# The first group's embedding product moved to the start of the program, and the last group's norm moved to VectorE

## The chip, the cores and the metric

The kernel runs on one core of a Trainium2 chip. The metric is the device time of one execution in microseconds (us). Times are medians over a few executions. The views of the trace below come from one profiled execution of the kernel before the change.

The engines are called PE (TensorE matmuls), PEld (its weight loads, which overlap with the matmuls), DVE (VectorE), ACT (ScalarE), POOL (GpSimd) and SP (SyncE, which here issues nearly all of the DMAs). TensorE runs at one of two clocks, 2.4 GHz or 1.2 GHz; the profile gives the granted share (1.00 or 0.50).

## The reference, cut to what matters

One layer on x with 2048 frames of 1024 features, all in float32:

```python
h = layer_norm(x)
q, k, v, gate, ... = split(h @ w_in)          # chunked attention and gated linear attention
mixer = concat(attention * silu, gla * silu) @ w_out
r = alpha * h + mixer
ple = p @ w_ple                               # "embedding product": p is 2048 x 256, w_ple 256 x 1024
y = r + sigmoid(r @ w_ple_gate + b) * ple
out = layer_norm(y)                           # "final norm"
```

The embedding product needs only the inputs p and w_ple. Its result is used at the end of the layer, in the gate.

## The kernel before

**Tiling.** The frames are cut into two superblocks (`sb` = 0, 1) of 1024 frames, and each into two groups (`g` = 0, 1) of 512. Everything is kept transposed, features on the partitions. A float32 product is made of three matmuls on parts of the operands: high by high, low by high, and high by low (`hh`, `hl` for the data, `whi`, `wlo` for the weights). A matmul has 128x512 columns, except for the last slabs of the last group, which have 256.

**Order.** For each superblock `gla_phase`, `attn_phase` and `out_phase` follow each other. The first `gla_phase` begins with `head()`, which norms the first x blocks, transposes them (`ln_T`: PE transposes, ACT evacuates as `t` on line 229, DVE splits into `hh` and `hl` on lines 151 and 152), and splits the first weight slabs. `out_phase` runs the output projection (slabs o0 to o7; the evacuation `ev_r` on lines 1171 to 1176 makes r and splits it), and then for each group the embedding product (48 matmuls with the left operands `whi` and `wlo` of two slabs of w_ple and the right ones `pTh`, `pTl`; evacuated as `ple` on line 1182) and eight gate slabs (`ev_y`, lines 1192 to 1201). `p_T(g)` loads p, transposes it with 8 PE transposes (line 1160) and splits it.

**Weights.** A slab is loaded raw by SP (`w_load`, `wraw`), cast to its high part by ACT (line 286) or DVE (line 284), and its low part is made by DVE (line 291). If the slab is used again, both parts go to DRAM (`wkept`) and are fetched from there later (`w_fetch`).

**What sets the order on an engine.** After every four matmuls `gemm` calls `tick()`, which runs evacuations that were put off and advances a "side" generator (`set_side`), whose `yield n` says after how many ticks it goes on. In `head()` and in the last slabs of the last group the order on DVE, ACT and POOL is the order in which the code is written (`manual_schedule`); elsewhere a scheduler orders the instructions. Each engine works in order. SP's DMAs use eight semaphores in turn, so each waits until the one eight places ahead of it has landed.

**The end.** `ln_last` is the final norm of the last group, which runs as a side generator beside the last slabs: transposes of the outputs `y`, statistics (line 414), scale and offset (lines 366, 367, 458, 474), stores. Some of its multiplications and additions run on POOL.

Of the kernel before, what the change touches and what calls it, by code (L numbers as in the profile page):

```python
# [26 lines left out]
F32 = mybir.dt.float32  # L27
# [17 lines left out]
def hymba_layer_kernel(  # L45
# [211 lines left out]
    def w_load(i, pool=pool_r, tag="r"):  # L257
        if i >= len(order) or i in wt or not first_use(i):
            return
        wt[i] = w_tile(pool, F32, i, "wraw", tag)  # L260
        queued.append(nc.sync.dma_start(wt[i], order[i]).ins)
# [73 lines left out]
    I = lambda *ns: [("i", n) for n in ns]  # L335
    for sb in range(NSB):
        keys += [("v", 0), ("v", 1)] + I(GQ, GK)
        keys += I(GV + 2, GV + 3, GQ + 1, GK + 1)
        keys += I(GG, GG + 1)
        for h in (0, 2):  # L340
            keys += I(*[n + h for n in (AK, AV, AV + 1, AQ, AG, AK + 1, AQ + 1, AG + 1)])
        keys += I(GG + 2, GG + 3)
        keys += [("o", k) for k in range(8)]
        for g in range(2):
            keys += [("e", 0), ("e", 1)] + [("g", k) for k in range(8)]
# [57 lines left out]
    def ln_last(sb, g, rows, ys, pst):  # L403
# [24 lines left out]
        def fin(b, hf, eng, mul=None):  # L428
            norm(b, hf)
            ln_store(sb, g, b, hf, y[b][hf], rows, eng, mul)  # L430

        for b in range(4):
            ps = pst(0)
            part(b, range(4), ps)
            nc.scalar.activation(y[b][0], ps, AF.Copy)
            yield 3
        yield 2
# [4 lines left out]
        yield 9  # L442
        for b in range(2):
            part(b, range(6, 8), pss[b])
            yield 1.5
        scale(0)
        yield 3
        fin(0, 1, nc.gpsimd)
        fin(0, 0, nc.gpsimd)
        yield 1  # L450
# [3 lines left out]
        fin(1, 0, nc.gpsimd, nc.gpsimd)  # L454
        yield 3.5
        norm(1, 1)
        yield 100
        TT = lambda eng, b, hf, i, op: eng.tensor_tensor(y[b][hf], y[b][hf], rows[2 * i + hf], op=op)
        for b in range(2, 4):
            part(b, [6], pss[b])  # L460
        TT(nc.vector, 1, 1, 0, OP.mult)
        for b in range(2, 4):
            part(b, [7], pss[b])
# [5 lines left out]
        TT(nc.gpsimd, 1, 1, 1, OP.add)  # L469
        ln_put(sb, g, 1, 1, y[1][1])  # L470
        for b in (1, 0):
            nc.scalar.activation(y[2 + b][0], y[2 + b][0], AF.Identity, bias=nm[:, b:b + 1], scale=r[:, b:b + 1])
# [4 lines left out]
        TT(nc.gpsimd, 3, 0, 0, OP.mult)  # L477
        TT(nc.vector, 2, 0, 0, OP.mult)
        TT(nc.vector, 2, 0, 1, OP.add)
        ln_put(sb, g, 2, 0, y[2][0])  # L480
        TT(nc.vector, 3, 0, 1, OP.add)
        ln_put(sb, g, 3, 0, y[3][0])
# [14 lines left out]
    khist = dram.tile([4, 2, 128, 512], F32, name="khist")  # L497
    vhist = dram.tile([2, 4, 2, 128, 512], F32, name="vhist")
# [12 lines left out]
    def gla_phase(sb):  # L511
# [234 lines left out]
        def head(idx):  # L746
# [34 lines left out]
            with tc.manual_schedule(engines={E.DVE, E.Activation, E.Pool}):  # L781
# [11 lines left out]
                w_split(0, "dve")  # L793
# [17 lines left out]
                w_split(2, "lo")  # L811
                w_split(3, "act")
                w_split(3, "lo")
                w_load(4)
                w_load(5)
# [324 lines left out]
    def out_phase(sb):  # L1140
# [66 lines left out]
        set_side(p_T(0), scale=3)  # L1207
        for s in range(0, 8, 2):
            for g in range(2):
                if s == 6 and g == 1 and nxt:  # L1210
                    xs = x_load(sb + 1, 0)
                for n in range(2):
                    gemm(wos[s + n], 8, 0, lambda k, g=g: (mh[k][g], ml[k][g]),
                         ev_r(s + n, g), g == 1)
        end_sides()
        end_pend()
        for g in range(2):
            pw = take(2)
            for s in range(8):
                gemm(pw[s // 4], 2, 2 * (s % 4), lambda k: pT[k], ev_ple(s), s % 4 == 3)  # L1220
# [7 lines left out]
            else:  # L1228
# [49 lines left out]
    edge["x"] = x_load(0, 1)  # L1278
# [65 lines left out]
```

## Time and profile before

| | before |
|---|---|
| median of 3 runs | 1376.54 us (1371.83 to 1377.86) |
| profiled execution | 1372.83 us |
| its span, first to last instruction | 1371.0 us |
| PE busy in the span | 1332.9 us (97%) |
| DVE busy, ACT busy | 739.2 us (54%), 562.1 us (41%) |
| mean granted TensorE clock | 0.992 |

The profiled execution's own time is 1.8 us more than its span, and it lies 3.7 us below the median of the three runs. The busy times say that PE works nearly without a pause; only where PE is idle, or at half clock, can time be won without taking work from it.

### The profile page before, as it was taken

Reading aid. Unit: us, or ns where it says so; the run is one execution under the profiler, and the core shown is the slowest. Engines: PE = TensorE matmul, PEld = TensorE weight load, DVE = VectorE, ACT = ScalarE, POOL = GpSimd, SP = SyncE. Lnnn points to the kernel's source line nnn. Section 1 sums busy time; section 2 is a strip of 40 time slices with the busy share of each in tenths; the row PEclk is TensorE's granted clock in tenths of the full one; section 3 lists DMA queues with packets and bytes.
Section 4 is the critical chain, followed back from the end, with each engine's and each line's share of the span. In section 5 each row is a group of like instructions: output and inputs, shape, how many; then the busy total and the mean of one; then the engine's idle time right before and its main releaser. Section 6 shows DMA issues by size and latency. Waiting matters only on the chain.

```text
span 1371.0 us, 21628 instructions
## 1 busy us (share of the span) xinstructions
PE 1332.9 (97%) x8440; PEld 1132.1 (83%) x8440; DVE 739.2 (54%) x1641; ACT 562.1 (41%) x1064; POOL 154.1 (11%) x233
## 2 busy tenths in 40 slices
PE   6999999999999999999999999999999999999995
PEld 5888888888888888888898988888888887888875
DVE  7755625554455745546884552455445555332286
ACT  4655525444454522524544542444344443112222
POOL 1000001211111100000100010121211120000012
PEclk9999999999999999999999999999999999999998
DMA  8360525241523335766613131322222213235551
GB/s 320 59 197 21 212 72 215 72 162 33 208 96 137 131 133 195 273 220 231 204 69 117 55 118 62 131 80 79 70 101 93 79 40 130 93 119 195 201 184 63
DMA packets 60271, 180.60 MB, mean 132 GB/s; under 512 B 6864, under 2 KB 8968, under 8 KB 60168
## 3 DMA queue, kind: packets, MB, share of 16 engines
q1 hardware_dynamic: 59648, 177.64, 36.9%
q10 hardware_dynamic: 520, 1.57, 1.1%
q8 instruction: 67, 1.10, 0.3%
q14 instruction: 36, 0.29, 0.1%
HBM read 116.14 MB, written 63.05 MB: 131 GB/s over the span
## 4 chain that ended last, share of the span: by engine, by line
PE 89%; DVE 5%; ACT 3%; DMA 1%; issue 1%; POOL 0%; SPq 0%; ACTq 0%; DVEq 0%; POOLq 0%
PE proj L317 56%; PE proj L917 7%; PE PT L1027 5%; PE PV L1050 5%; PE proj L557 5%; PE S L994 3%; PE S L992 2%; PE O L704 1%; DMA wraw<-in_wi_dram 1%; PE kvp L657 1%; PE O L700 1%; DVE ysb L397 1%; PE CN L679 1%; PE CN L317 0%; DVE ysb L399 0%
## 5 line engine op out<-in xcount | busy, mean ns | idle before, releaser
L317 PE MATMUL proj<-hh,whi 128*128 128x512 f32 (+1 forms) x912 | 358.4, 393 | 1.3 <-ACT glr L574 0.7
L317 PE MATMUL proj<-hh,wlo 128*128 128x512 f32 (+1 forms) x912 | 357.3, 392 | 0.0
L317 PE MATMUL proj<-hl,whi 128*128 128x512 f32 (+1 forms) x912 | 353.7, 388 | 0.0
L317 PEld LDWEIGHTS proj<-hh,whi 128*128 128x128 f32 x912 | 172.5, 189 | 30.3 <-issue 1.0
L317 PEld LDWEIGHTS proj<-hl,whi 128*128 128x128 f32 x912 | 172.4, 189 | 29.4
L317 PEld LDWEIGHTS proj<-hh,wlo 128*128 128x128 f32 x912 | 172.3, 189 | 29.1
L1002 ACT ACTIVATE P<-P,s 128x640 f32<-128x640 f32 (+4 forms) x128 | 97.5, 761 | 159.6 <-DVE s L1001 101.3
L1010 POOL TENSOR_SCALAR P<-P,s 128x640 f32<-128x640 f32 (+4 forms) x128 | 96.1, 750 | 486.5 <-DVE s L1009 393.7
L998 DVE CUSTOM_DVE_ANT_0 P<-S,bias 128x640 f32<-128x640 f32 (+4 forms) x128 | 94.7, 740 | 103.8 <-PE S L994 100.6
L317 PE MATMUL proj<-mh,whi 128*128 128x512 f32 x256 | 99.9, 390 | 0.0
L317 PE MATMUL proj<-mh,wlo 128*128 128x512 f32 x256 | 99.6, 389 | 0.0
L159 POOL TENSOR_TENSOR rstd<-v,nhalf 128x1 f32<-128x1 f32 (+2 forms) x44 | 33.2, 761 | 573.7 <-DVE v L157 524.9
L1027 PE MATMUL PT<-ident,P 128*128 128x128 f32 x560 | 83.8, 276 | 0.0
L291 DVE TENSOR_TENSOR wlo<-wraw,whi 128x1024 fp32r<-128x1024 f32 (+1 forms) x46 | 56.0, 1224 | 49.7 <-ACT whi L286 48.1
L1032 ACT ACTIVATE PT<-PT 128x384 f32<-128x384 f32 (+2 forms) x128 | 59.3, 464 | 50.8 <-PE PT L1027 50.1
L1027 PEld LDWEIGHTS PT<-ident,P 128*128 128x128 f32 x560 | 65.3, 140 | 14.2 <-issue 5.1
L317 PE MATMUL proj<-ml,whi 128*128 128x512 f32 x192 | 75.1, 391 | 0.0
L557 PE MATMUL proj<-whi,hl 128*128 128x272 f32 (+1 forms) x256 | 74.7, 296 | 0.0
L557 PE MATMUL proj<-whi,hh 128*128 128x272 f32 (+1 forms) x256 | 74.0, 296 | 0.7 <-ACT glr L574 0.7
L917 PE MATMUL proj<-whi,hh 128*128 128x256 f32 x256 | 74.4, 291 | 0.0
L888 DVE SCALAR_TENSOR_TENSOR ql<-proj,qh 64x512 fp32r<-64x512 f32 x64 | 44.0, 688 | 53.2 <-ACT qh L885 51.5
L917 PE MATMUL proj<-wlo,hh 128*128 128x256 f32 x256 | 72.3, 283 | 0.0
(216 smaller groups left out, 2389.9 us busy)
## 6 DMA issues: line engine op xcount, KB each, us to landing
whi<-wkept SPq DMA_DIRECT2D x64, 512.0 KB, 3.6
wlo<-wkept SPq DMA_DIRECT2D x64, 512.0 KB, 4.4
wkept<-whi SPq DMA_DIRECT2D x44, 512.0 KB, 2.7
wkept<-wlo SPq DMA_DIRECT2D x44, 512.0 KB, 3.3
wraw<-in_wi_dram SPq DMA_DIRECT2D x26, 512.0 KB, 5.1
x<-in_x_dram SPq DMA_DIRECT2D x32, 256.0 KB, 5.7
out_dram<-ysb SPq DMA_DIRECT2D x32, 256.0 KB, 2.1
bias<-relrows SPq DMA_DIRECT2D x32, 144.0 KB, 2.8
```

What stands on the lines that cost most here:

```text
L291: nc.vector.tensor_tensor(lo, raw, hi.bitcast(F32), op=OP.subtract)
L317: nc.tensor.matmul(ps[:, cols], lhsT=l[:, c0 + k, :], rhs=rhs(k)[m][:, cols], start=(j == 0), stop=(j == n - 1))
L557: nc.tensor.matmul(ps[:, c0:c0 + nw], lhsT=h[k][g][:, b * 128:(b + 1) * 128], rhs=W[k // 4][m][:, k % 4, :], start=(n == 0), stop=(n == 23))
L888: nc.vector.scalar_tensor_tensor(ql[h][o, :], ps[r, :], QSCALE, qh[h][r, :].bitcast(F32), op0=OP.mult, op1=OP.subtract)
L917: nc.tensor.matmul(ps[:, bb * 256:bb * 256 + 256], lhsT=h[k][g][:, c], rhs=W[k // 4][m][:, k % 4, :], start=(k == 0 and n == 0), stop=(k = ...
L994: nc.tensor.matmul(ps[:, d0:d0 + n1], lhsT=ll, rhs=kt[:, c0:c0 + n1], start=False, stop=True)
L998: nc.vector.tensor_tensor_reduce(P[:, :ncol], ps[:, 512 - n_prev:512 + n_cur], bias[pr, h][:, 640 - ncol:640], 1.0, -3e38, OP.add, OP.max, ...
L1002: nc.scalar.activation(P[:, :ncol], P[:, :ncol], AF.Exp, bias=s4[:, 1:2], scale=1.0, accum_out=s4[:, 2:3])
L1010: nc.gpsimd.tensor_scalar(P[:, :ncol], P[:, :ncol], s4[:, 3:4], 1.0, op0=OP.mult, op1=OP.mult)
L1027: nc.tensor.transpose(ps[:, b, :], P[:, (b0 + b) * 128:(b0 + b + 1) * 128], ident)
L1032: nc.scalar.activation(pt[:, ks, cs], ps[:, :nb, :], AF.Copy)
L1050: nc.tensor.matmul(pv[r, qp * 256 + c0:qp * 256 + c1], lhsT=V[pr, gi][:, kb * 128 + 64 * h:kb * 128 + 64 * h + 64], rhs=pt[h][:, b - k0, c ...
```

## The change

The change has three parts.

1. **Start.** The embedding product of superblock 0, group 0 becomes the first work of the program. p of this group (two DMAs of 256 KB) and the two slabs of w_ple (now also under the key "f") are loaded ahead of and between the x blocks. `head()` first splits p and w_ple, then runs eight products of six matmuls each; the norm, transposes and splits of the first two x blocks (`first()`) run as their side generator. ACT evacuates each of the eight results, and SP stores it to DRAM (`pled`, 256 KB each). ACT instead of DVE now casts the first v slab. The raw loads of the slabs GQ and GK and of the second group's x are issued later on SP.
2. **Middle.** In `out_phase` of superblock 0, `p_T(0)` and the 48 matmuls of group 0 are gone. Eight loads bring `ple` back from DRAM; SP issues them behind the eight loads of the next x. The w_ple slabs are first used under "e" at group 1, so the raw load, split and store that stood at group 0 now stand there.
3. **End.** In `ln_last` all scale and offset work is on DVE, none on POOL. Its start is put off from 32 to 35, and its pauses (`yield`) become shorter.

```diff
+    slab.update({("f", k): wple[k] for k in range(2)})
+    keys += [("f", 0), ("f", 1)]
...
-            keys += [("e", 0), ("e", 1)] + [("g", k) for k in range(8)]
+            keys += [("e", k) for k in range(2) if sb or g] + [("g", k) for k in range(8)]
...
-        def fin(b, hf, eng, mul=None):
+        def fin(b, hf):
             norm(b, hf)
-            ln_store(sb, g, b, hf, y[b][hf], rows, eng, mul)
+            ln_store(sb, g, b, hf, y[b][hf], rows, nc.vector)
...
-            yield 3
-        yield 2
+            yield 2.4
...
-        yield 9
+        yield 4.4
         for b in range(2):
             part(b, range(6, 8), pss[b])
-            yield 1.5
+            yield 0.8
         scale(0)
         yield 3
-        fin(0, 1, nc.gpsimd)
-        fin(0, 0, nc.gpsimd)
-        yield 1
+        for b in range(2):
+            fin(b, 1)
+            yield 1.5
+        for b in range(2):
+            fin(b, 0)
+            yield 1.8
...
-        fin(1, 0, nc.gpsimd, nc.gpsimd)
-        yield 3.5
-        norm(1, 1)
         yield 100
...
-        TT(nc.gpsimd, 3, 0, 0, OP.mult)
-        TT(nc.vector, 2, 0, 0, OP.mult)
-        TT(nc.vector, 2, 0, 1, OP.add)
...
+        for b in range(2, 4):
+            TT(nc.vector, b, 0, 0, OP.mult)
+            TT(nc.vector, b, 0, 1, OP.add)
...
+            def p_T():
+
+                for k in range(2):
+                    ps = bank()
+                    for b in range(4):
+                        nc.tensor.transpose(ps[:, b * 128:(b + 1) * 128],
+                                            edge["p0"][b // 2][:, b % 2 * 256 + k * 128:b % 2 * 256 + k * 128 + 128],
+                                            ident)
+                    pT[k] = U("pTh", F32R), U("pTl", F32R)
+                    nc.scalar.activation(pT[k][0], ps, AF.Copy)
+                    nc.vector.tensor_tensor(pT[k][1], ps, pT[k][0].bitcast(F32), op=OP.subtract)
+
+            def ev_f(s):
+                def ev(ps):
+                    t = U("ple")
+                    nc.scalar.activation(t, ps, AF.Copy)
+                    nc.sync.dma_start(pled[s], t)
+                return ev
...
+                w_split(F[1], "lo")
+                w_load(idx[3])
+                edge["x"] = x_load(0, 1)
+                w_split(V[0], "act")
+                yield
                 for k, _ in enumerate(ln_T(0, xs, bank, range(0, 2))):
                     if k == 1:
-                        w_split(1, "act")
-                w_split(0, "lo")
-                w_split(1, "lo")
-                w_split(2, "act")
+                        w_split(V[1], "act")
+                    if k == 4:
+                        w_split(V[0], "lo")
+                    yield
+
+            with tc.manual_schedule(engines={E.DVE, E.Activation, E.Pool}):
+                w_split(F[0], "dve")
+                p_T()
+                w_split(F[0], "lo")
+                w_load(idx[2])
+                w_split(F[1], "act")
+                set_side(first(), delay=-1)
+                for s in range(8):
+                    gemm(F[s // 4], 2, 2 * (s % 4), lambda k: pT[k], ev_f(s), False, lo_last=True)
+                end_sides()
+                end_pend()
+                for f in F:
+                    del wt[f]
+                w_split(V[1], "lo")
+                w_split(idx[2], "act")
...
-        set_side(p_T(0), scale=3)
+        if sb:
+            set_side(p_T(0), scale=3)
...
                     xs = x_load(sb + 1, 0)
+                    if sb == 0:
+                        for k in range(8):
+                            ple[k] = U("ple")
+                            nc.sync.dma_start(ple[k], pled[k])
...
-            pw = take(2)
-            for s in range(8):
+            pw = take(2) if sb or g else []
+            for s in range(8 if pw else 0):
                 gemm(pw[s // 4], 2, 2 * (s % 4), lambda k: pT[k], ev_ple(s), s % 4 == 3)
...
-                    set_side(ln_last(sb, 1, rows, ys[1], bank), delay=32, carry=True)
+                    set_side(ln_last(sb, 1, rows, ys[1], bank), delay=35, carry=True)
...
+    edge["f"] = take(2)
+    edge["p0"] = [U("praw"), U("praw")]
+    for j in range(2):
+        nc.sync.dma_start(edge["p0"][j].rearrange("t (b d) -> t b d", b=2),
+                          p[j * 256:(j + 1) * 256, :].rearrange("(b t) d -> t b d", t=128))
+    w_load(0)
     edge["x0"] = x_load(0, 0, range(0, 2))
-    w_load(0)
     w_load(1)
-    w_load(2, pool_w, "w")
+    w_load(2, pool_t)
+    w_load(3, pool_t)
     edge["x0"] += x_load(0, 0, range(2, 4))
-    w_load(3)
...
-    edge["x"] = x_load(0, 1)
```

The following rows show where the change puts instructions. In them a line number belongs to the kernel that the row is of; the changed kernel's lines are later by some (line 286 is its line 290, line 291 its 295).

On ACT at the start of the program, before the change (x are the normed x halves, t the evacuated transposes, `whi` of 1088 columns a cast of a v slab):

```order
L197 ACTIVATE x<-x,nmr_177,rstd 128x512
L197 ACTIVATE x<-x,nmr_187,rstd 128x512
L229 ACTIVATE t<-O_193,vecs 128x256
L229 ACTIVATE t<-tp,vecs 128x256
L286 ACTIVATE whi<-wraw 128x1088
```

And with the change (`pTh` is p's high part, `whi` of 1024 columns the second w_ple slab's, `ple` an evacuation of the product):

```order
L794 ACTIVATE pTh<-O_156 128x512
L794 ACTIVATE pTh<-tp 128x512
L290 ACTIVATE whi<-wraw 128x1024
L197 ACTIVATE x<-x,nmr_197,rstd 128x512
L800 ACTIVATE ple<-proj 128x512
L197 ACTIVATE x<-x,nmr_217,rstd 128x512
L800 ACTIVATE ple<-proj 128x512
L290 ACTIVATE whi<-wraw 128x1088
L800 ACTIVATE ple<-proj 128x512
L229 ACTIVATE t<-O_263,vecs 128x256
L800 ACTIVATE ple<-proj 128x512
L229 ACTIVATE t<-O_282,vecs 128x256
```

The first normed half of x now stands behind p's two evacuations and the cast of the second w_ple slab, and the evacuations of the product stand between the x work.

On PE in the output projection of superblock 0 with the change, between its last slab but one and its last one for group 1 (`mh`, `ml`, `mlp` are the mixer's parts; before the change the two slabs follow each other with nothing between, and the transposes of praw and x come later, beside the product and the gate slabs):

```order
L321 MATMUL proj<-mh,whi 128x512
L321 MATMUL proj<-ml,whi 128x512
L321 MATMUL proj<-mh,wlo 128x512
L1207 MATMUL tq<-ident,praw 128x128 x8
L226 MATMUL tq<-ident,x 128x128 x4
L321 MATMUL proj<-mh,whi 128x512
L321 MATMUL proj<-mlp,whi 128x512
L321 MATMUL proj<-mh,wlo 128x512
```

The eight transposes of group 1's p and four transposes of the next superblock's x, one from each of its four blocks, moved ahead of the last slab.

On DVE beside the last half slabs, before the change (`ysb` is the final norm's output, `rows` its scale and offset rows, `y` a gate slab's output, `bst` the statistics):

```order
L179 SCALAR_TENSOR_TENSOR nmr2_13057<-bmv2_13050,rstd_13055 128x2
L366 TENSOR_TENSOR ysb_12848<-ysb_12848,rows_12517 128x512
L366 TENSOR_TENSOR ysb_12847<-ysb_12847,rows_12515 128x512
L414 BN_STATS bst8_12845<-tq_13083 128x6 x2
L414 BN_STATS bst8_12846<-tp_13088 128x6 x2
L1193 SCALAR_TENSOR_TENSOR t_13106<-t_13106,ple_12509 128x256
L1196 SCALAR_TENSOR_TENSOR y_12689<-t_13106,y_12689 128x256
```

And with the change:

```order
L1243 SCALAR_TENSOR_TENSOR y_12580<-t_13059,y_12580 128x256
L372 TENSOR_TENSOR ysb_12893<-ysb_12893,rows_12550 128x512
L373 TENSOR_TENSOR ysb_12893<-ysb_12893,rows_12554 128x512
L372 TENSOR_TENSOR ysb_12895<-ysb_12895,rows_12550 128x512
L373 TENSOR_TENSOR ysb_12895<-ysb_12895,rows_12554 128x512
L372 TENSOR_TENSOR ysb_12892<-ysb_12892,rows_12548 128x512
L373 TENSOR_TENSOR ysb_12892<-ysb_12892,rows_12552 128x512
L1240 SCALAR_TENSOR_TENSOR t_13100<-t_13100,ple_12533 128x256
L1243 SCALAR_TENSOR_TENSOR y_12654<-t_13100,y_12654 128x256
L372 TENSOR_TENSOR ysb_12894<-ysb_12894,rows_12548 128x512
L373 TENSOR_TENSOR ysb_12894<-ysb_12894,rows_12552 128x512
L420 BN_STATS bst8_12890<-tq_13120 128x6 x2
```

Where DVE had two multiplications of the final norm (POOL had the rest of that pair of blocks), it now has all eight instructions, six of them ahead of the y of the second half slab.

## Rows read from the trace of the kernel before

**Rows 1.** The page: busy time, share of the span and instructions of each engine.

```profile
PE 1332.9 (97%) x8440; PEld 1132.1 (83%) x8440; DVE 739.2 (54%) x1641; ACT 562.1 (41%) x1064; POOL 154.1 (11%) x233
```

**Rows 2.** Windows of the first 31 us (the columns are in the first row).

```profile
core 0: us, PE busy (x) PEld busy (x) DVE busy (x) ACT busy (x) POOL busy (x), PEclk, DMA share, GB/s
0.00:10.40 10.40, 0.00 (x1) 0.00 (x1) 4.70 (x16) 2.10 (x2) 3.25 (x11) 1.00 0.72 254
10.40:17.44 7.04, 6.34 (x26) 5.46 (x27) 6.04 (x15) 5.32 (x9) 1.72 (x5) 1.00 0.83 294
17.44:27.68 10.24, 8.19 (x61) 7.29 (x60) 9.13 (x20) 3.76 (x5) 1.10 (x2) 1.00 0.95 350
27.68:31.09 3.41, 2.92 (x13) 2.92 (x14) 2.91 (x8) 2.50 (x8) 0.00 (x0) 0.50 1.03 414
```

**Rows 3.** Waits in the first 45 us (total, times, longest).

```profile
PE O L226 <- ACT x L197: 12.3, 4, 10.4
...
PE CN L317 <- ACT whi L286: 1.0, 1, 1.0
```

**Rows 4.** Timeline of DVE, start and length, then SP's issues of the v slabs.

```profile
19.15 2.48 DVE L291 TENSOR_TENSOR wlo<-wraw,whi 128x1088 fp32r<-128x1088 f32 x2
21.55 1.28 DVE L187 BATCH_NORM_STATS2 bst<-x 128x6 f32<-128x512 f32 x2
...
3.06 0.91 SPq L261 DMA_DIRECT2D wraw<-in_wv_dram  x2
...
wraw<-in_wv_dram SPq DMA_DIRECT2D x2, 544.0 KB, 7.0
```

**Rows 5.** Groups of instructions in the first 45 us (count, busy, mean ns of one).

```profile
L197 ACT ACTIVATE x<-x,nmr,rstd 128x512 f32<-128x512 f32 x11 | 8.4, 808 | 16.1 <-DVE nmr L179 15.8 <-DMA wraw<-in_wi_dram 0.4
...
L152 DVE TENSOR_TENSOR hl<-t,hh 128x256 fp32r<-128x256 f32 x16 | 6.8, 426 | 0.6
...
L229 ACT ACTIVATE t<-O,vecs 128x256 f32<-128x256 f32 x11 | 5.9, 568 | 2.1 <-PE O L226 1.8
...
L286 ACT ACTIVATE whi<-wraw 128x1024 fp32r<-128x1024 f32 x2 | 2.1, 1054 | 0.5 <-DMA wraw<-in_wi_dram 0.5
```

**Rows 6.** The product's window (its 48 matmuls alone), and its evacuations, 540 to 569 us.

```profile
557.20:568.10 10.90, 10.80 (x48) 8.60 (x47) 1.00 1.00 361
...
L1182 ACT ACTIVATE ple<-proj 128x512 f32<-128x512 f32 x7 | 4.2, 596 | 3.4 <-PE proj L317 3.4
```

**Rows 7.** Timeline: transposes of p at 475 us, then ACT and DVE around 552 us.

```profile
475.35 0.60 PE L1160 MATMUL tq<-ident,praw 128*128 128x128 f32 x4
...
552.06 1.04 ACT L286 ACTIVATE whi<-wraw 128x1024 fp32r<-128x1024 f32 x1
...
553.27 0.68 DVE L1171 SCALAR_TENSOR_TENSOR t<-hh,proj 128x512 f32<-128x512 f32 x1
...
554.02 0.16 DVE L212 SCALAR_TENSOR_TENSOR nmr<-bmv,rstd 128x1 f32<-128x1 f32 x1
```

**Rows 8.** Windows of the end (columns as in rows 2).

```profile
1328.80:1331.60 2.80, 0.33 (x4) 0.09 (x3) 2.73 (x6) 0.00 (x0) 0.00 (x0) 0.99 0.49 187
1331.60:1335.00 3.40, 3.40 (x16) 3.40 (x17) 1.49 (x6) 0.60 (x1) 0.00 (x0) 0.50 0.00 0
...
1345.00:1354.50 9.50, 9.50 (x82) 9.50 (x81) 5.46 (x18) 3.80 (x7) 1.98 (x2) 1.00 0.01 3
```

**Rows 9.** Timeline of DVE, POOL and PE at the end.

```profile
1349.42 0.43 DVE L1196 SCALAR_TENSOR_TENSOR y<-t,y 128x256 f32<-128x256 f32 x1
...
1353.23 3.17 POOL L367 TENSOR_TENSOR ysb<-ysb,rows 128x512 f32<-128x512 f32 x2 [1.81 <-DVE ysb L366]
...
1354.42 0.28 PE L317 MATMUL proj<-hh,wlo 128*128 128x256 f32 x1
...
1358.12 1.37 DVE L1196 SCALAR_TENSOR_TENSOR y<-t,y 128x256 f32<-128x256 f32 x1
...
1365.28 2.68 DVE L458 TENSOR_TENSOR ysb<-ysb,rows 128x512 f32<-128x512 f32 x3 [0.32 <-ACT ysb L472]
```

More of the change, by code (lines that the diff above doesn't have):

```diff
@@ L259, in w_load @@
             return
-        wt[i] = w_tile(pool, F32, i, "wraw", tag)
+        if pool is pool_t:
+            t = pool_t.tile([128, 6, 256], F32, name="wraw", tag="t").rearrange("p a b -> p (a b)")
+            wt[i] = t[:, 0:w_cols(i)].rearrange("p (k c) -> p k c", c=order[i].shape[2])
+        else:
+            wt[i] = w_tile(pool, F32, i, "wraw", tag)
         queued.append(nc.sync.dma_start(wt[i], order[i]).ins)
@@ L453, in ln_last @@
             part(b, range(4, 6), pss[b])
-        fin(1, 0, nc.gpsimd, nc.gpsimd)
-        yield 3.5
-        norm(1, 1)
         yield 100
         TT = lambda eng, b, hf, i, op: eng.tensor_tensor(y[b][hf], y[b][hf], rows[2 * i + hf], op=op)
[L459 to L463, printed above, removed]
+        for k in (6, 7):
+            for b in range(2, 4):
+                part(b, [k], pss[b])
         mv, r = pair_stat(st[2:])
@@ L468, in ln_last @@
         nm = pair_nm(mv, r)
-        TT(nc.gpsimd, 1, 1, 1, OP.add)
-        ln_put(sb, g, 1, 1, y[1][1])
-        for b in (1, 0):
+        for b in range(2):
             nc.scalar.activation(y[2 + b][0], y[2 + b][0], AF.Identity, bias=nm[:, b:b + 1], scale=r[:, b:b + 1])
@@ L476, in ln_last @@
             ln_put(sb, g, 2 + b, 1, y[2 + b][1])
-        TT(nc.gpsimd, 3, 0, 0, OP.mult)
-        TT(nc.vector, 2, 0, 0, OP.mult)
-        TT(nc.vector, 2, 0, 1, OP.add)
-        ln_put(sb, g, 2, 0, y[2][0])
-        TT(nc.vector, 3, 0, 1, OP.add)
-        ln_put(sb, g, 3, 0, y[3][0])
+        for b in range(2, 4):
+            TT(nc.vector, b, 0, 0, OP.mult)
+            TT(nc.vector, b, 0, 1, OP.add)
+            ln_put(sb, g, b, 0, y[b][0])
     def silu_evac(ps, k, g, first):
@@ L497, in hymba_layer_kernel @@
     khist = dram.tile([4, 2, 128, 512], F32, name="khist")
+    pled = dram.tile([8, 128, 512], F32, name="pled")
     vhist = dram.tile([2, 4, 2, 128, 512], F32, name="vhist")
@@ L779, in side, with first @@
                     yield 2
-            with tc.manual_schedule(engines={E.DVE, E.Activation, E.Pool}):
+            F = edge["f"]
+            V = idx[:2]
+            pT = {}
+            def p_T():
[14 more added lines that the diff above has]
+                return ev
+            def first():
                 st = [x_stat(xs, (b,)) for b in range(2)]
@@ L792, in head @@
                 x_half(xs[1][1], r, nm, 0, nc.vector)
-                w_split(0, "dve")
+                yield
+                w_split(F[1], "lo")
+                w_load(idx[3])
+                edge["x"] = x_load(0, 1)
+                w_split(V[0], "act")
+                yield
                 for k, _ in enumerate(ln_T(0, xs, bank, range(0, 2))):
                     if k == 1:
-                        w_split(1, "act")
-                w_split(0, "lo")
-                w_split(1, "lo")
-                w_split(2, "act")
+                        w_split(V[1], "act")
+                    if k == 4:
+                        w_split(V[0], "lo")
+                    yield
+            with tc.manual_schedule(engines={E.DVE, E.Activation, E.Pool}):
[13 more added lines that the diff above has]
+                w_split(idx[2], "act")
                 st = [x_stat(xs, (b,)) for b in (2, 3)]
@@ L810, in head @@
                 x_half(xs[3][1], *v, 0, nc.vector)
[L811 to L815, printed above, removed]
+                w_split(idx[2], "lo")
+                w_split(idx[3], "act")
+                w_split(idx[3], "lo")
+                w_load(idx[3] + 1)
+                w_load(idx[3] + 2)
                 set_side(side(), delay=8, scale=0.9)
```

## The prediction

> **What bounds the kernel now.** I began with the busy times by engine, because they say which engine the work belongs to: PE is busy in 1332.9 of 1371.0 us, DVE in 739.2 and ACT in 562.1 [rows 1]. So 48 matmuls less in the middle are worth their time there, and work put into an idle stretch of PE is free as long as it delays nothing else. PE has idle stretches in two places that this change touches, the start and the end, so I read these in windows.
>
> In the first 10.40 us PE does one instruction; then it needs 6.34 of 7.04 us, 8.19 of 10.24, and 2.92 of 3.41 at half clock [rows 2]. The list of waits says what PE lacks first: 10.4 us at a stretch for the first normed x on ACT [rows 3]. From 17.44 to 27.68 DVE is busy for 9.13 of 10.24 us [rows 2]: after its empty beginning the start is set by DVE's splits, not by PE. The mark that I follow is the end of the low part of the second v slab, with which the first products on v can run: 19.15 + 2.48, and the next DVE work starts at 21.55 [rows 4].
>
> At the end there are 2.47 us without PE work from 1328.80 to 1331.60, then 3.40 us at half clock [rows 8]. The last matmul starts at 1354.42, but the last y ends only at 1358.12 + 1.37 = 1359.49 [rows 9]: behind the last matmul DVE sets the time.
>
> **The middle: what the change takes away.** The 48 matmuls of the product take 10.80 of a window of 10.90 us [rows 6], 0.227 us each, with PE full. The eight transposes of p go too: four are busy for 0.60 us with overlap [rows 7], so about 0.4 us in the stream for four, 0.8 for eight. That is -11.7 us.
>
> Against this stands a new wait. The changed order puts the transposes of the next x ahead of the last output slab. Before, the product starts at about 557.1, so the last slab (24 x 0.227 = 5.45 us) at 551.7; with p's transposes gone the slab before it ends at 550.9. The transpose of the fourth x block needs its norm on ACT, which now stands behind the weight cast (1.04 [rows 7]) and two evacuations of p (0.60 each, as the same shape in [rows 6]), and takes 0.81 [rows 5]: 554.0. The slab behind it needs a free result bank, that is DVE's evacuation of the slab two before it (0.68 [rows 7]), which now stands behind the statistics of all x blocks (the last of them ends at 554.18 before [rows 7], some 0.8 earlier now) and a weight split (1.24 [rows 4]): 553.4 + 1.24 + 0.68 = 555.3 at most, 554.9 if the x loads land a little sooner. PE has its 12 transposes done at about 552.3. Wait: 2.6 us, with 0 (ACT and DVE both early) and 3.0 as bounds. After waits of that size TensorE ran at half clock: 3.41 us [rows 2] and 3.40 us [rows 8], each 1.7 us of work lost. I count half of that, 0.8. Middle: -11.7 + 2.6 + 0.8 = **-8.3** (-11.7 to -7.0).
>
> At no cost I count the eight loads of `ple` (2 MB behind x's 2 MB on SP, used only by the first gate slab over 5 us later; DMA moved 361 GB/s in the product's window [rows 6]) and w_ple's raw load and split at group 1 instead of its fetch, 2 x 1.05 us on ACT and 2 x 1.24 on DVE beside a full PE. At group 0 the same casts and the stores of 2 MB fall away. If the loads came late, the first gate slab would wait up to 5 us.
>
> **The start: what is added.** Queue by queue. **SP:** p (0.52 MB) and the first w_ple slab (0.52 MB) now stand ahead of x, and the second slab ahead of the v slabs. Before, x and both v slabs (2.16 MB) had landed by 3.97 + 7.0 = 11.0 us [rows 4]. The second w_ple slab is now 2.62 MB deep in the queue; at 294 to 350 GB/s [rows 2] that is 11.0 + 1.3 to 1.6 = 12.3 to 12.6. **ACT:** the cast of that slab stands ahead of the first x norm. From 12.3 on ACT has, up to the last transposed t: one cast 1.05, two norms at 0.81, seven evacuations at 0.60, two casts of v slabs at 1.05 to 1.12, eight t at 0.57: 1.05 + 1.62 + 4.2 + 2.2 + 4.56 = 13.6 us [rows 5, 6], to 25.9 without a gap. **DVE:** behind the last t come one split pair (about 0.7, its second instruction 0.43 [rows 5]) and the low part of v (1.24): 27.9 at the earliest. The low part of the first v slab stands in the middle of the pairs and leaves two or three of them behind (another 1.3). Gaps on ACT are likely too: each evacuation waits for its six matmuls, with two result banks in turn, and these wait for the bank. Walking through the order with these waits I get 30.4. The mark moves from 21.55 to 27.9 to 30.4, so by +6.3 to +8.8. DVE and ACT behind the mark have the same work as before, so all moves by as much, except that the slab GK is no longer late (PE waited 1.0 us for its cast [rows 3]): **+7.8**, bounds +5.3 and +8.8. POOL has only its small reciprocal roots there as before. The eight stores of `pled` stand ahead of some loads on SP, each waiting for its evacuation; GK and the second group's x, issued between them, are needed over 10 us later, by 35 us, so I count nothing.
>
> So the product costs 7.8 us at the start instead of 10.9: the 10.4 us in which PE has no work are mostly time in which the data isn't there either.
>
> TensorE's clock weighs on this: the stretch behind waits ran at 0.50 [rows 2], and the new product starts after an idle beginning and stops at each evacuation. The Trainium skill (TensorE: Matmul & The Clock Gate, "A second HAM failure mode: psum-queue depth-cycling") says that a matmul stream that idles briefly between groups as it cycles through its PSUM banks makes the clock swing between its levels. By that the product would run at 0.454 us a matmul, 21.8 us instead of 10.9. Rows bear it out only in part, since one such stretch is 3.41 us. It is the second rival.
>
> **The end.** The norm's start is put off, so that PE's four transposes no longer stand before a y that isn't there. Of the 2.47 us idle I expect 1.2 to stay and the half clock (1.7 us of work [rows 8]) to go: 1.3 + 1.7 = 3.0. But DVE now has eight scale and offset instructions (0.68 each for this shape, as [rows 7]) instead of two: 4.1 us more in the window from 1345.0 to 1354.5, where it has 9.5 - 5.46 = 4.04 free [rows 8]. It is just full, and the transposes of the second half slab wait behind it for about 1.2. Last matmul: -1.8. Behind it POOL no longer works beside DVE. There a DVE instruction of 128x256 took 1.37 us, with POOL idle 0.43 [rows 9]; the last two pairs shrink from 4.9 us to about 1.7, the last y by another 3.2. From the last y to the end some 8.5 us stay, less about 1.1 for the slowed small ones. Sum -6.1; as DVE has no slack, I take **-5.5** (-3 if DVE's queue delays the last two slabs' y by 2.5 more, -6.5).
>
> **Sum.** +7.8 - 8.3 - 5.5 = **-6.0 us**, on the profiled 1372.83: 1366.8. The median of three lies 3.7 above the profiled execution, so on its scale 1370.5; I say 1370.
>
> **Rivals.**
> *No stall in the middle.* If the x statistics and casts are early enough, 3.4 us come back: -9.4, 1363.4 profiled, 1367 as a median. For it: DVE and ACT are half idle there. Against: the order has the casts ahead. The same size comes with an ACT without gaps at the start (-8.5). Together 0.32.
> *The start is dearer.* The product runs largely at half clock and ACT waits for it: mark at 34.5, +12.0, sum -1.8: 1371.0 profiled, 1374.7 as a median. For it: the half clock in the rows. Against: product and x work alternate, so PE's slowness hides partly behind ACT. Chance 0.20.
> *Slower: the x work stands behind the product.* If the alternation fails, so that the product, started at about 9, runs for its 21.8 us first, the mark comes 11.1 us later (from the first transpose at 10.4 to 21.55 now): 42, +19.5 net, sum +5.7: 1378.5 profiled, 1382 as a median. It turns slower where the mark is later than 21.55 + 1.0 + 13.8 = 36.4. Against: ACT's order has the x norms between the first evacuations. Chance 0.10.
> *The forecast* itself has 0.38.
>
> **Numbers.** 0.5% (6.9 us) is about what a measurement of this kernel tells from no change. Beyond it lie the first rival (0.32) and of the forecast, whose sum falls short by 0.9, a third (0.12): faster 0.44. Within it: the rest of the forecast, the dearer start and a third of the slower rival: 0.49. Slower 0.07. The range goes from the first rival with all terms at their good ends (-12: 1364, less 3 for the runs' own spread) to the dearer start with the same spread: 1361 to 1378.
>
> **What would show it.** Right: the mark at 28 to 31 us; ACT nearly without idle time from 12 to 26; PE idle for 2 to 3 us just before the last output slab, near 553; no half clock near 1332; 128x256 instructions of DVE at 0.43 to the end; the last y 5 us earlier. Wrong: a mark later than 36; long waits of the first gate slab for `ple`; PE waiting for y in the last half slabs.

## The result, and the profile after

| | before | with the change |
|---|---|---|
| median (runs) | 1374.29 us (1371.05 to 1377.86, 6) | 1366.89 us (1365.58 to 1368.39, 6) |
| profiled execution, its span | 1372.83, 1371.0 us | 1367.03, 1364.9 us |
| mean granted clock | 0.992 | 0.996 |

The ratio is 0.995, with a 95% interval of 0.9931 to 0.9969: faster by 0.3 to 0.7%. The span fell by 6.1 us; the sum in the prediction was -6.0. The text below asks whether the terms are as good as the sum.

The simplest way to find where the time went is to look up the same instruction in both traces and to note how much later it stands. These are four instructions of ACT and the last one of DVE. Between the second row and the third the difference first rises to +6.51 (465 us) and then falls by 0.97, because p's transposes for group 0 are gone; this fall belongs to the middle.

| stretch | same instruction, start before and after (us) | later by |
|---|---|---|
| start | weight cast, 83.68 and 91.05 | +7.37 |
| behind the start | key/value evacuation, 103.23 and 109.09 | +5.86 |
| to the last output slabs | r's high part, 531.45 and 536.99 | +5.54 |
| middle | `ysb` of the last group but one, 1318.50 and 1318.62 | +0.12 |
| end | DVE's last instruction ends, 1367.96 and 1361.86 | -6.10 |

**The start.** The windows below are of the changed kernel; the columns are busy us (and instructions) of PE, PEld, DVE, ACT and POOL, the granted clock, the DMA share and GB/s. Ahead of 13.91 us the trace has no record of the clock, and the column then says 1.00.

```profile
0.00:10.40 10.40, 4.00 (x12) 2.60 (x13) 4.98 (x10) 2.48 (x3) 3.58 (x13) 1.00 0.77 252
10.40:13.91 3.51, 3.51 (x10) 2.43 (x8) 3.44 (x9) 1.06 (x2) 0.58 (x1) 1.00 1.02 405
13.91:20.00 6.09, 5.55 (x27) 4.04 (x26) 3.69 (x10) 5.94 (x10) 0.80 (x1) 1.00 0.93 318
20.00:26.00 6.00, 6.00 (x36) 5.12 (x35) 2.94 (x8) 4.81 (x10) 0.00 (x0) 1.00 1.01 334
```

Against [rows 2], PE works for 4.00 of the first 10.4 us instead of standing idle, and from 13.91 to 26 it is busy for 11.55 of 12.09 us, ACT for 10.75. The trace records full clock from 13.91 on. Ahead of that matmuls of 128x512 follow each other at 0.43 us, and later at 0.23, so the first ones ran at half clock. The timeline of DVE and ACT in the same stretch (start, length; in brackets the idle time before it and what ended it):

```profile
7.53 0.69 DVE L288 CAST whi<-wraw 128x1024 fp32r<-128x1024 f32 x1 [3.29 <-DMA wraw<-in_wple_dram]
...
9.78 1.21 DVE L295 TENSOR_TENSOR wlo<-wraw,whi 128x1024 fp32r<-128x1024 f32 x1
10.91 1.28 DVE L187 BATCH_NORM_STATS2 bst<-x 128x6 f32<-128x512 f32 x2
...
28.67 1.28 DVE L295 TENSOR_TENSOR wlo<-wraw,whi 128x1088 fp32r<-128x1088 f32 x1
29.87 1.28 DVE L187 BATCH_NORM_STATS2 bst<-x 128x6 f32<-128x512 f32 x2
...
42.44 2.47 DVE L187 BATCH_NORM_STATS2 bst<-x 128x6 f32<-128x512 f32 x4
...
11.90 1.06 ACT L290 ACTIVATE whi<-wraw 128x1024 fp32r<-128x1024 f32 x1 [5.02 <-DMA wraw<-in_wple_dram]
13.91 0.81 ACT L197 ACTIVATE x<-x,nmr,rstd 128x512 f32<-128x512 f32 x1 [0.95 <-DVE nmr L179]
```

The mark of the prediction, the end of the second v slab's low part, stands at 29.87 (21.55 in [rows 4]), 8.3 us later. The second w_ple slab landed at 11.9, the first slab at 7.5.

**The middle.** PE's longest wait behind the start is there. First the list of waits of PE (total, times, longest), then the timeline of PE, DVE and ACT around it, then the window behind it:

```profile
PE tq L226 <- ACT x L215: 3.5, 2, 3.0
...
557.11 1.04 PE L1207 MATMUL tq<-ident,praw 128*128 128x128 f32 x8
558.88 0.33 PE L226 MATMUL tq<-ident,x 128*128 128x128 f32 x1 [0.52 <-ACT x L215]
562.20 0.33 PE L226 MATMUL tq<-ident,x 128*128 128x128 f32 x1 [2.99 <-ACT x L215]
562.39 0.50 PE L321 MATMUL proj<-mh,whi 128*128 128x512 f32 x1
...
554.00 0.69 DVE L205 BATCH_NORM_STATS2 bst<-x 128x6 f32<-128x512 f32 x1 [1.94 <-DMA x<-in_x_dram]
554.62 0.14 DVE L212 SCALAR_TENSOR_TENSOR nmr<-bmv,rstd 128x1 f32<-128x1 f32 x1
...
560.51 1.23 DVE L295 TENSOR_TENSOR wlo<-wraw,whi 128x1024 fp32r<-128x1024 f32 x1 [1.45 <-ACT whi L290]
561.66 0.68 DVE L1218 SCALAR_TENSOR_TENSOR t<-hh,proj 128x512 f32<-128x512 f32 x1
...
554.84 4.70 ACT L215 ACTIVATE x<-x,nmr,rstd 128x512 f32<-128x512 f32 x6 [6.34 <-DVE nmr L212]
559.44 1.04 ACT L290 ACTIVATE whi<-wraw 128x1024 fp32r<-128x1024 f32 x1
560.39 1.06 ACT L1210 ACTIVATE pTh<-tq 128x512 fp32r<-128x512 f32 x2
561.35 1.51 ACT L215 ACTIVATE x<-x,nmr,rstd 128x512 f32<-128x512 f32 x2
...
563.45:566.87 3.42, 3.42 (x10) 2.64 (x9) 2.73 (x6) 1.26 (x2) 0.17 (x1) 0.50 1.00 305
```

PE's wait ends with the norm of the fourth x block on ACT, behind six norms, the cast and two evacuations of p, and is followed by 3.42 us at half clock.

**The end.** Windows of the changed kernel that answer to [rows 8], and DVE's last two y's, which answer to [rows 9]:

```profile
1328.80:1331.60 2.80, 1.88 (x16) 1.65 (x15) 2.73 (x6) 0.00 (x0) 0.00 (x0) 1.00 0.49 187
1331.60:1335.00 3.40, 3.30 (x28) 3.30 (x29) 2.30 (x9) 0.96 (x2) 0.00 (x0) 1.00 0.03 5
1345.00:1354.50 9.50, 7.54 (x60) 6.90 (x59) 8.84 (x20) 4.08 (x7) 0.00 (x0) 1.00 0.29 112
...
1350.65 0.33 PE L418 MATMUL tq<-ident,y 128*128 128x128 f32 x1 [1.13 <-DVE y L1243]
...
1353.09 0.42 DVE L1243 SCALAR_TENSOR_TENSOR y<-t,y 128x256 f32<-128x256 f32 x1
...
1354.25 0.42 DVE L1243 SCALAR_TENSOR_TENSOR y<-t,y 128x256 f32<-128x256 f32 x1
```

PE's idle time near 1330 fell from 2.5 to 0.9 us, and the half-clock stretch is gone. DVE is nearly full from 1345 to 1354.5 (8.84 of 9.50), and one transpose waits 1.13 us for a y. The last y ends at 1354.67 instead of 1359.49.

### The profile page after: what moved, and what is told of

It is laid out like the page before. It is cut to its first block, busy times and chain, and to the rows that moved or that the text cites. A ratio compares the mean times of both kernels' runs of the same rounds, so it can differ in the third digit from the quotient of the medians.

```text
span 1364.9 us, 21668 instructions
## 1 busy us (share of the span) xinstructions
PE 1333.0 (98%) x8440; PEld 1128.7 (83%) x8440; DVE 741.0 (54%) x1649; ACT 563.7 (41%) x1066; POOL 146.0 (11%) x227
## 4 chain that ended last, share of the span: by engine, by line
PE 87%; DVE 6%; ACT 4%; DMA 1%; issue 1%; POOL 0%; SPq 0%; ACTq 0%; DVEq 0%; POOLq 0%
PE proj L321 55%; PE proj L964 7%; PE PV L1097 5%; PE PT L1074 5%; PE proj L557 4%; PE S L1041 3%; PE S L1039 2%; PE O L704 1%; DMA wraw<-in_wi_dram 1%; DVE wlo L295 1%; PE kvp L657 1%; PE O L700 1%; DVE ysb L403 1%; DVE bst L187 1%; PE CN L679 1%
## 5 line engine op out<-in xcount | busy, mean ns | idle before, releaser
L290 ACT ACTIVATE whi<-wraw 128x1024 fp32r<-128x1024 f32 (+1 forms) x47 | 49.4, 1059 | 62.2 <-PE proj L321 50.0
```

What stands on the lines that cost most here:

```text
L290: nc.scalar.activation(hi, raw, AF.Copy)
```

## The experiments

Each run is named by its label. Where a ratio to the kernel before stands, it has its 95% interval. "The difference" is, as in the table above, how much later an instruction stands than in the trace of the kernel before.

**The three parts alone.** Three kernels made from the one before, each with one part of the change.

The start alone (group 0's product stays in the middle as well). The lines are against the changed kernel; they and the `ln_last` of before, left out here, take the other two parts back:

```diff
+            keys += [("e", 0), ("e", 1)] + [("g", k) for k in range(8)]
...
+        set_side(p_T(0), scale=3)
...
+            pw = take(2)
```

> The kernel before with the first part of the change alone: the product of group 0 is done at the start and its result stored, but the middle does that product again as before, and the end is as before. Own theory: the start delays all that follows by the same amount as in the changed kernel (+7.4 us up to 99 us, +5.9 from 103 us on, where one half-clock stretch falls away), and nothing gives it back: span 1371.0 + 5.9 = 1376.9. Rival (the delay is DMA time that the rest can take up): less than +2 left at 540 us.

Measured: median 1379.4 us against 1373.53, ratio 1.0047 (1.0029 to 1.0065); span 1378.4. The same ACT instructions stand 8.3 us later at 84 us, 6.85 later from 104 us on and 6.8 to 7.3 later from there to 1318. Nothing gives the delay back (+6.83 at 540 us); the rival is out. The start costs 5.9 us in the medians.

The end alone (the diff of `ln_last` as it stands in the change, with the start put off to 35), of which these lines stand for the whole:

```diff
-                    set_side(ln_last(sb, 1, rows, ys[1], bank), delay=32, carry=True)
+                    set_side(ln_last(sb, 1, rows, ys[1], bank), delay=35, carry=True)
...
-        fin(1, 0, nc.gpsimd, nc.gpsimd)
...
+            TT(nc.vector, b, 0, 0, OP.mult)
+            TT(nc.vector, b, 0, 1, OP.add)
```

> The kernel before with the third part alone (start of the last norm put off, shorter pauses, all scale and offset work on VectorE). Own theory: the parts don't act on each other, so the span falls by the 6.2 us that the two traces show behind 1320 us: 1364.8. Rival: part of the gain came from the earlier parts, less than 4 us here.

Measured: median 1366.48, ratio 0.995 (0.9932 to 0.9969), span 1364.2; an ACT instruction at 1311.52 stands 0.57 us earlier, one at 1363.73 stands 6.45 earlier. So the end alone gives 5.9 between these two, as much as in the whole change.

The middle alone:

```diff
+            keys += [("e", k) for k in range(2) if sb or g] + [("g", k) for k in range(8)]
...
+                            nc.sync.dma_start(ple[k], x[k * 128:(k + 1) * 128, 0:512])
...
+            for s in range(8 if pw else 0):
```

> The kernel before with the second part alone. The product of group 0 is left out altogether (no matmuls for it anywhere), and rows of x are loaded in the place of its result, by eight loads of the same size. Own theory: PE's order moves the transposes ahead of the last output slab here too, so PE waits 3 to 3.5 us there and then runs 3.4 us at half clock; of the 11.7 us only about 6.4 are won: span 1364.6. Rival (the wait comes from the later start): the middle gives 11 or more, span 1360 or less.

Measured: median 1366.64, ratio 0.9947 (0.9927 to 0.9966), span 1363.5. The difference goes from +0.99 at 440 us to -6.06 at 663 us: 7.05 won of 11.7. The wait is there without the new start, and of nearly the same length (3.5 in the changed kernel):

```profile
PE tq L226 <- ACT x L215: 3.3, 2, 3.0
```

The rival (the later start makes the wait) is out. Over the three the medians differ by +5.9, -7.0 and -6.9 from before, together -8.1 (before rounding); the whole change measured -7.4. The parts add up within what the runs scatter.

**The wait in the middle.** The loads moved behind the output projection:

```diff
         end_sides()
         end_pend()
+        if sb == 0:
+            for k in range(8):
+                ple[k] = U("ple")
+                nc.sync.dma_start(ple[k], pled[k])
```

> The changed kernel with one edit: the eight loads of the stored product are written behind the output projection instead of ahead of its last two slabs. With it PE's order has the transposes of p and x behind the last output slab, as before the change. Own theory: the wait of 3.5 us and the half-clock stretch (1.7 us of work) fall away: span 1364.9 - 5 = 1360, and the first gate slab doesn't wait for the loads. Rival (DMA is full there, and the loads now come too late): the first gate slab's evacuation waits 3 to 6 us for them, and the span stays within 2 us of 1364.9.

Measured: median 1362.08 us (1361.25 to 1364.4), ratio 0.9924 (0.99 to 0.9948), which is 4.8 below the changed kernel's 1366.89. PE's list of waits has no entry from 540 to 640 us, and the two windows that had the wait and the half clock are full:

```profile
553.00:560.00 7.00, 7.00 (x32) 5.80 (x31) 5.34 (x13) 2.08 (x3) 1.01 (x2) 1.00 0.66 211
560.00:567.00 7.00, 7.00 (x32) 5.82 (x31) 6.35 (x17) 6.46 (x10) 1.80 (x5) 1.00 0.36 140
```

In this trace the middle gives 11.8 us (from +9.41 at 464 us to -2.37 behind 750): all of the 11.7 that the removed work is worth. The rival (late loads) is out: the loads landed between 571 and 577 us, and nothing waited for them. The span, 1362.4, came down by 2.5 only, because in this execution the start cost more: data landed 0.8 us later, PE waited 2.9 instead of 1.6 us near 105 us, and a half-clock stretch followed that the changed kernel's profile doesn't have (108.27 to 111.69). That is scatter of the same start program, and the medians are the better measure: the spans of the other five executions are 1359.2 to 1360.2, those of the changed kernel 1363.5 to 1365.5.

**The end, taken apart.** The eight instructions of the four `fin` calls on GpSimd (program order as in the change):

```diff
-            ln_store(sb, g, b, hf, y[b][hf], rows, nc.vector)
+            ln_store(sb, g, b, hf, y[b][hf], rows, nc.gpsimd)
```

> The changed kernel, but the eight scale and offset instructions of the first two blocks of the last norm (those of the four fin calls) run on GpSimd; their place in the program, the later start and the shorter pauses stay. Own theory: VectorE beside a working GpSimd is slow again (1.4 us instead of 0.43 for 128x256), GpSimd needs 8 x 1.4 = 11 us from 1345.7 on, the last two slabs' y fall into that, and the last y comes 3 to 5 us later than at 1354.7: span up by 3 to 5, 1368 to 1370. Rival (the gain at the end is that of the later start and shorter pauses): span within 1.5 us of 1364.9, for VectorE gets 5.5 us of work less in a window that is just full.

Measured: median 1370.4, 3.5 above the changed kernel; span 1368.5. Only the additions ran on POOL, since `ln_store` leaves the multiplications on DVE; so this moved four instructions, not the eight that the expectation speaks of. The timeline of DVE and POOL, then the wait of PE, then a window:

```profile
1348.03 1.48 DVE L1240 SCALAR_TENSOR_TENSOR t<-t,ple 128x256 f32<-128x256 f32 x1
1349.54 1.37 DVE L1243 SCALAR_TENSOR_TENSOR y<-t,y 128x256 f32<-128x256 f32 x1
...
1345.83 4.80 POOL L373 TENSOR_TENSOR ysb<-ysb,rows 128x512 f32<-128x512 f32 x3 [1.87 <-DVE ysb L372]
...
PE tq L418 <- DVE y L1243: 3.9, 1, 3.9
...
1350.84:1354.25 3.41, 3.29 (x16) 3.29 (x17) 1.69 (x7) 0.47 (x1) 1.28 (x1) 0.50 0.36 133
```

Beside POOL the 128x256 instructions take 1.4 us again. The price doesn't fall on the last two y's, as expected, but on an earlier one, for which PE waits 3.9 us and then runs at half clock. The span went up by 3.6, in the forecast 3 to 5; the rival is out. Ahead of the end this execution stood 0.7 us earlier than the changed kernel's, so the end itself took 4.2 us more.

The start of the last norm put off by 32 instead of 35:

```diff
-                    set_side(ln_last(sb, 1, rows, ys[1], bank), delay=35, carry=True)
+                    set_side(ln_last(sb, 1, rows, ys[1], bank), delay=32, carry=True)
```

> The changed kernel with one number changed: the last norm's start put off by 32 ticks again instead of 35. Own theory: PE's fourth transpose stands again in front of a y that isn't there, so PE waits about 2.5 us near 1329 instead of 1.0, and then runs a stretch of 3.4 us at half clock (1.7 us of work): last matmul 2 to 3 us later, span 1367 to 1368. Rival (VectorE's full queue sets the end, whatever PE does): span within 1 us of 1364.9.

Measured: median 1367.84, span 1366.6. The last gate evacuations and the end stand 1.6 us later than in the changed kernel, with the difference ahead of the end at +0.07. PE waits 2.5 us instead of 1.0, but no half-clock stretch follows:

```profile
PE tq L418 <- DVE y L1248: 2.5, 1, 2.5
```

So the wait itself returned and was passed on whole; of the 3 us that I gave the later start, the half clock's part doesn't belong to it alone. The 1.6 us lie between the theory's 2 to 3 and the rival's 1.

**The start, taken apart.** Four runs' marks are measured from the end of the first w_ple slab's low part, so that the landing of the data drops out. In the changed kernel it is 29.87 - 10.91 = 18.96, and in three further executions with the same start also 18.96.

Every second evacuation on VectorE:

```diff
+                    if s % 2:
+                        nc.vector.tensor_copy(t, ps)
+                    else:
+                        nc.scalar.activation(t, ps, AF.Copy)
```

> The changed kernel, but every second of the eight evacuations of the product at the start runs on VectorE instead of ScalarE. Own theory: from 12 to 26 us ScalarE's queue sets the pace of the transposed x; it loses 4 x 0.6 = 2.4 us, VectorE has that much free. The mark (end of the low part of the second v slab, 29.87 in the changed kernel) comes 1.5 to 2.4 us earlier, measured from the end of the first w_ple slab's low part (10.91) so that the landing of the data doesn't count: 16.6 to 17.5 instead of 18.96. Rival (PE's product at 1.2 GHz or its two result banks set the pace): mark within 0.5 us.

Measured: median 1368.71 us (1366.46 to 1371.36), ratio 0.9967 (0.9951 to 0.9982), so no gain against the changed kernel's 1366.89; mark 30.76 - 10.97 = 19.79, later by 0.8. The theory fails: ACT now waits 2.6 us for PE in this stretch instead of 1.1, and the last copy on DVE stands directly ahead of the second v slab's low part, with which the mark ends; it accounts for 0.6 of the 0.8. The rival, a mark within 0.5 us, fails too:

```profile
ACT t L229 <- PE O L226: 2.6, 3, 1.7
...
28.96 0.68 DVE L801 COPY ple<-proj 128x512 f32<-128x512 f32 x1
29.56 1.28 DVE L295 TENSOR_TENSOR wlo<-wraw,whi 128x1088 fp32r<-128x1088 f32 x1
30.76 1.28 DVE L187 BATCH_NORM_STATS2 bst<-x 128x6 f32<-128x512 f32 x2
```

The same copies together with the loads moved as in e4 (the two diffs above):

> The changed kernel with both edits: the loads of the stored product behind the output projection, and every second evacuation at the start on VectorE. Own theory: the gains add up, 5 us in the middle (median 1362 as measured with the first edit alone) and 1.5 to 2.4 us at the start: median about 1360, the fastest of all. Rival (the start's gain is taken up by the loads of the next weights that the same stretch waits for): median as with the first edit alone.

Measured: median 1363.33 (1361.45 to 1365.44), against 1362.08 with the moved loads alone; mark 31.73 - 11.98 = 19.75. The copies give nothing here either. The two runs with the copies, e7 and this one, differ by the moved loads alone, and their medians by 5.4 us: the gain of e4 once more.

So PE rather than ACT? The next run relieves PE, by shorter matmuls:

```diff
+            cc = slice(0, 128) if lo_last and 0 < j < n - 1 else cols
+            nc.tensor.matmul(ps[:, cc], lhsT=l[:, c0 + k, :], rhs=rhs(k)[m][:, cc],
```

> The changed kernel, but in each of the eight products at the start four of the six matmuls have 128 instead of 512 columns (that part of the product is left out; order and count of the instructions stay). The mark again from the end of the first w_ple slab's low part: 18.96 us in the changed kernel, where PE has no gap from 14.8 to 26.2 and ScalarE waits 1.1 us. Theory now: PE sets the pace there, and ScalarE is close behind: PE loses 24 x 0.17 = 4 us, ScalarE's queue then takes over, mark 1 to 2 us earlier (17 to 18). Rival (ScalarE's queue sets the pace, as in my prediction): mark within 0.5 us of 18.96. Second rival (PE alone): 15.

Measured: 29.86 - 11.41 = 18.45, earlier by 0.5: at the first rival's edge and short of the theory's 1 to 2. The kernel ran once (1368.74 us), and so did the next one (1368.45), so their times decide nothing; the marks are read from their traces. Windows of this run:

```profile
13.91:18.67 4.76, 3.39 (x14) 3.10 (x15) 3.10 (x8) 4.08 (x6) 0.80 (x1) 1.00 0.92 308
...
20.00:26.00 6.00, 5.31 (x39) 4.63 (x38) 3.66 (x10) 5.77 (x12) 0.00 (x0) 1.00 0.99 311
```

From 20 to 26 us ACT is full now (5.77 of 6.00), and PE has gaps. The clock rose later, too: the first record of full clock stands at 18.67 us, where the changed kernel has 13.91. Part of the relief may have gone there; how much, no run shows.

The shorter matmuls together with the copies on VectorE (the diffs of e9 and e7):

> The edit of the run before (four of six matmuls of the product at the start cut to 128 columns) and every second evacuation on VectorE. Theory now (PE first, ScalarE close behind): with both relieved the mark comes earlier than with either alone, 2 to 4 us before the changed kernel's 18.96 (15 to 17), though the copies alone made it 0.8 later. Rival (VectorE's own work or the landing of the v slabs sets the mark): no better than with the shorter matmuls alone.

Measured: 31.64 - 11.88 = 19.76. With both relieved it is no better than with the copies alone, and worse than with the shorter matmuls alone; the rival's forecast holds. Full clock is recorded from 20.13 on, PE waits twice for a copy on DVE, and the last copy is again ahead of the mark. So none of the three edits brought the mark earlier by more than 0.5 us. With PE relieved ACT was full, and with the copies on DVE the last of them stood ahead of the mark. Which engine sets the pace in the changed kernel itself these runs don't separate, since e7 and e10 added work to DVE and in e9 and e10 the clock rose later.

## Why the prediction was right, and which of its steps were not

**The sum.** -6.0 forecast, -6.1 in the spans, -7.4 in the medians. That it came out to 0.1 us is luck. In the spans the start cost 1.3 us less than forecast (+6.5 at 465 us instead of +7.8), the middle gave 1.9 less (-6.4 instead of -8.3) and the end 0.7 more (-6.2 instead of -5.5), and these cancel. One addition was wrong: the good ends of all terms give 5.3 - 11.7 - 6.5 = -12.9, not -12, which hardly moves the range.

**The start, +7.8 with bounds +5.3 and +8.8.** Measured +7.37 at 84 us, mark +8.3 (forecast +6.3 to +8.8, walked through 30.4 against 29.87). The landing of the second w_ple slab (12.3 to 12.6; 11.9) and the norm behind it nearly held, and PE's wait for GK's cast is gone from the list. That ACT's queue sets the pace, as the forecast had it, is shown only in half: ACT was busy for 10.75 of 12.09 us from 13.91 to 26, but PE was busy for 11.55, since only the first 12 of the 48 matmuls ran ahead of the x work (from 8.37 us on), at half clock, and the other 36 (36 x 0.23 = 8.3 us) share the stretch with it. e7, e9 and e10 fit engines that are close to a tie there, but don't separate them. What I didn't see was a gain behind the start: with the later and denser start PE waited 1.6 instead of 2.5 us at 97 to 105 us, and the half-clock stretch at 99 us, 1.5 us of loss, didn't come, which left +5.9. This isn't sure to happen, and it isn't the change's merit: e4 and e6 have the same start and the stretch at 108 us, and e2, which has the start of the kernel before, waited 2.5 us as that kernel did, and the stretch didn't follow. What decides it from execution to execution stays open. The landing of the first w_ple slab doesn't decide it alone: it came at 7.50 us in the changed kernel, and at 8.29 both in e4, with the stretch, and in e5, without it.

The rival with the dearer start fails: the clock reached 1.00 at 13.91 and stayed there to 563 us. The slower rival (mark at 42) fails too, for the x work ran between the product's evacuations. The Trainium skill (TensorE: Matmul & The Clock Gate, "A second HAM failure mode: psum-queue depth-cycling") let one expect a clock that swings while the product cycles through its banks; this trace doesn't agree, for the product's two banks had PE gaps of 0.2 and 0.5 us behind its first matmul, and no half clock was recorded from 13.91 to 563 us.

**The middle, -8.3 with bounds -11.7 and -7.0.** In the profiled execution p's transposes gave -0.97 (the difference falls from +6.51 at 465 us to +5.54 at 482 us) and the rest -5.43: -6.4, outside the bounds. The place was right: the transposes moved ahead of the last output slab, and PE waited there. Two terms were mis-sized: the wait was 3.5 us instead of 2.6, and the half clock, which I counted by half, came whole (1.7 instead of 0.8).

The chain was right only in part. In the forecast the wait ended with DVE's evacuation of a result bank (554.9), 0.9 us behind the fourth block's norm on ACT (554.0). In the trace PE waits for that norm, which begins at 561.35; the transpose runs at 562.20. The bank's evacuation, behind a weight split as forecast, ends at 561.66 + 0.68 = 562.34, level with it, and PE's list has no wait for it. The step that failed lies ahead of both: I let ACT's cast begin when the slab before had ended. That slab ended at about 557.1, and the cast began at 559.44, for six norms of x stood ahead of it (4.70 us). These had begun late, since DVE works in order and the first block's nmr stood behind the statistics of a half that landed only at 553.98.

This is one execution, and six others have the same order of PE at this place. The table compares them; the last column is the change of the difference from 440 to 750 us.

| run | fourth x load took | PE's wait | half clock behind or in it | middle |
|---|---|---|---|---|
| changed kernel | 5.74 us | 3.5 us | 3.4 us | -6.4 us |
| e9 | 5.74 | 3.5 | 6.8 | -5.7 |
| e3 | 5.49 | 3.3 | 3.4 | -7.0 |
| e10 | 4.22 | 2.5 | 3.4 | -8.0 |
| e5 | 4.13 | 3.0 | 3.4 | -7.2 |
| e7 | 4.06 | 3.0 | 3.4 | -7.3 |
| e6 | 4.04 | 2.5 | none | -9.3 |

e6's wait, and the window from its end on, at full clock:

```profile
PE tq L226 <- ACT x L215: 2.5, 1, 2.5
...
563.93:570.00 6.07, 6.07 (x27) 5.03 (x28) 4.55 (x9) 2.21 (x4) 0.64 (x2) 1.00 0.99 322
```

So the middle is worth 5.7 to 9.3 us from one execution to the next, and the forecast lies inside that; where the fourth load of x was quick, the wait was shorter. In e6 the start cost 3.0 us more than in the changed kernel's profile, and behind the middle less than 0.1 of it was left, because the wait was shorter there and no half clock followed. Why the load is quick in one execution and not in another stays open. The loads of the stored product aren't needed for it: it took 5.62 us in e4, where they come later, and 4.20 in the kernel before and 5.74 in e1, which have none. e3 shows the wait without the new start, and e4 shows it gone with PE's old order, with a slow load all the same. The rival without a wait (-11.7) was thus one edit away.

**The end, -5.5 with bounds -3 and -6.5.** Measured -6.2 (from +0.12 to -6.10). PE's idle time near 1330: 1.0 stayed (1.2 forecast). DVE was just full, and one transpose waited 1.13 (1.2). The last y came 4.8 earlier (5.0), and from there to DVE's end 7.2 us instead of 8.5 (7.4 forecast). I had taken -5.5 for caution and the walked value of -6.1 was the better one. e5 shows that POOL's work beside DVE costs, e6 that the later start is worth 1.6 us. Part of the -6.2 belongs to the execution that was profiled before the change: e3 ends as that kernel does and waits the same 2.5 us near 1325, no half clock followed, and its end took 1.5 us less.

**At no cost** I had counted the loads, the later weight fetches and POOL; no wait in the list of the changed kernel contradicts that.

## What to carry to other kernels

Work that is moved into an engine's idle beginning is free only for the time in which its data is there and the others' isn't: here 12 of 48 matmuls ran ahead of the x work. Where a scheduler sets the order, look at what it moved to the place that you emptied: with eight loads written two slabs too early, twelve transposes stood ahead of a slab, the last two waited for x, and 4.8 us of 11.7 were lost. And where two engines both look like the pace-maker, relieving one by loading a third doesn't tell which it is.

## What the runs showed of the hardware that was not expected

Shorter matmuls did not bring full clock sooner: with four of six cut to 128 columns, it is first recorded from 18.67 and 20.13 us on (e9, e10), with the whole product between 12.70 and 16.05 in seven executions (13.91 in the changed kernel).

And a wait of PE isn't always followed by half clock, even with the same instructions around it. At the end, with three transposes ahead of a wait of 2.5 us and one behind it, it came before the change [rows 8] and in e1, and not in e3 and e6. In the middle, with a wait of 2.5 us in both, it came in e10 (0.50 from 562.85 to 566.26) and not in e6. What decides it stays open.
